# Fifteen 1 MB weight buffers instead of six of 2 MB, in a decoder block with 32 experts

## The chip, the cores and the metric

The kernel runs on one core of one Trainium2 chip. The metric is the device time of one execution in microseconds (us), as the median of several runs.

## What is computed

One decoder block on 512 tokens of width 2048, all in float32. Two attention branches (forgetting attention and chunkwise retention, 8 heads of 128 each) are merged through gates and projected back; a router then picks for each token one group of four, and two of the eight experts in it; each expert is a gated MLP; the sum is normalized. The part that matters here:

```python
h = h + merged @ w_out[l]
hn = rmsnorm(h, norm_ffn_w[l]).reshape(b * s, d)
...
def expert_block(args):
    xi, e = args
    return (jax.nn.silu(xi @ w1[e]) * (xi @ w3[e])) @ w2[e]

yb = lax.map(expert_block, (xb, blk_expert)).reshape(cap, d) * buf_w[:, None]
return jnp.zeros((t_tok + 1, d), h.dtype).at[buf_tok].add(yb)[:t_tok]
...
h = h + moe.reshape(b, s, d)
return rmsnorm(h, norm_final_w)
```

For each expert w1 and w3 are 2048 x 512 and w2 is 512 x 2048, 4 MB each, so the 32 experts have 403 million bytes of weights. The program reads all of them.

## The kernel before

**First stage.** The projections, the branches and the output projection take 120 weight units of 1 MB (128 partitions x 2048 floats). `Stream.unit` loads two units at a time, 2 MB with rows of 16 KB, into one of two buffers of the pool `raw` (L74). ScalarE casts a unit to the high part of a split number (L96), VectorE subtracts to get the low part (L97), both into one of two buffers of 2 MB of the pool `split`; TensorE multiplies high and low parts against activations that are split in the same way (L225 to L244, L477, L593 to L595).

**Router.** The rows of h are transposed and split once more into `hh` and `hl` (L552, L553), TensorE makes the logits from them (L557 the high part, L558 the low), and a chain of small instructions on all engines gives every token its experts and places. `prep` then gathers the tokens of an expert by matmuls with a selection matrix (L720) and writes them to `xs`.

**Expert stage.** An expert has six pieces of 2 MB: four for `gemm1`, each with four k tiles of w1 and of w3 (two rows of 8 KB in a partition), and two for `gemm2`, each with two column blocks of w2 (rows of 16 KB). The program runs gemm1 of expert e, the gather for e + 1, and gemm2 of e - 1, in that order. The pieces go in turn through six buffers: the two of `raw`, the two of `split`, and two of a new pool `raw2`. All loads are issued by SyncE (SP) at L817, in the order in which the program writes them (`manual_schedule` for SP): a load whose buffer is not free holds up all that stand behind it. The other engines are ordered by the scheduler. The result of an expert, 64 rows, goes to `ybuf` in memory with a scatter from GpSimd (L798); the last expert's result stays on chip as `ys`, and `fw` is the final norm's weight on all partitions.

**Combine.** For each of four tiles of 128 tokens SP loads both expert rows of each token from `ybuf` (L925, 2 MB with rows of 16 KB, into the same six buffers). TensorE adds h, the second row and the last expert's (L938 to L941), VectorE adds the first row (L942, and L945 the second row for one column block) into a tile `res`, of which there are two, in the buffers of `raw2`. Then comes the norm: squares on ScalarE (L947), sums and inverse root on VectorE (L951 and L952, L112 to L122), scaling (L957 on VectorE, L959 on ScalarE), and two writes to the output (L962).

After that comes a loop for experts with more than 64 tokens, which calls the same functions.

## Time and profile before

| | us |
|---|---|
| runs, median (lowest to highest of 3) | 2464.65 (2463.22 to 2465.13) |
| profiled execution, whole time | 2461.32 |
| its span in the profile | 2459.5 |
| TensorE busy | 2355.6, 96% of the span |
| VectorE busy | 737.6, 30% |
| ScalarE busy | 488.6, 20% |
| GpSimd busy | 233.4, 9% |
| data moved, whole span | 594.22 MB, mean 242 GB/s |

The busy shares are means over the two stages, the seam at some 1423 to 1454 us between them, and the combine from some 2414 us on, so each stage has to be read by itself. The slices of the page show this at once: data move at 73 to 154 GB/s in slices 2 to 23, and at 414 to 423 in slices 25 to 39. The granted TensorE clock is 0.99 of full speed over the span.

### The profile page before, as it was taken

The numbers are of one execution on the slowest core, as the hardware profiler recorded it, in microseconds if no ns is written. First come the engines' busy times: TensorE is split into PE (matmuls) and PEld (weight loads), VectorE is DVE, ScalarE is ACT, GpSimd is POOL, SyncE is SP. The second block draws the span as 40 slices with busy tenths as digits, with TensorE's granted clock in tenths as the row PEclk, the third lists the DMA queues.
The fourth block names the chain that finished last, engine by engine and source line by source line (L and its number), as shares of the span: only waits on it lengthen the run. The fifth ranks groups of instructions, "written<-read, shape, count | busy, mean of one in ns | idle before, by whom it ended". The sixth has DMA issues, their size and how long they took to land. (4 is left out here: it accounts for less than half of the span.)

```text
span 2459.5 us, 35971 instructions
## 1 busy us (share of the span) xinstructions
PE 2355.6 (96%) x16110; PEld 1605.8 (65%) x16114; DVE 737.6 (30%) x1271; ACT 488.6 (20%) x617; POOL 233.4 (9%) x328
## 2 busy tenths in 40 slices
PE   8999999999999999999999979999988999999986
PEld 6888888888888888888888854544444444444422
DVE  4444445544442222244433231111111111111105
ACT  5222223222222222232223310000010000000013
POOL 0000000100100000001003121111111111111002
PEclk9999999999999999999999989999999999999998
DMA  7233334232223333244432369999999999999996
GB/s 289 98 107 128 108 101 139 79 110 73 107 78 128 128 124 117 109 151 154 146 125 87 146 267 416 414 421 422 422 421 422 422 422 422 421 422 422 422 423 249
DMA packets 85839, 594.22 MB, mean 242 GB/s; under 512 B 7800, under 2 KB 24248, under 8 KB 34640
## 3 DMA queue, kind: packets, MB, share of 16 engines
q1 hardware_dynamic: 56704, 549.48, 55.1%
q0 software_dynamic: 7856, 25.61, 3.1%
q10 hardware_dynamic: 21120, 16.78, 2.1%
q8 instruction: 128, 2.10, 0.3%
q14 instruction: 31, 0.25, 0.0%
HBM read 562.72 MB, written 37.24 MB: 244 GB/s over the span
## 5 line engine op out<-in xcount | busy, mean ns | idle before, releaser
L745 PE MATMUL ab<-wraw,xs 128*64 128x512 f32 x2048 | 461.8, 603 | 39.2 <-DMA wraw<-in_wM_dram 39.0
L225 PE MATMUL acc<-xh,whl 128*128 128x512 f32 x1152 | 453.2, 393 | 0.0
L227 PE MATMUL acc<-xh,whl 128*128 128x512 f32 x1152 | 453.2, 393 | 0.0
L226 PE MATMUL acc<-xl,whl 128*128 128x512 f32 x1152 | 452.7, 393 | 0.0
L96 ACT CAST whl<-wraw 128x2048 fp32r<-128x2048 f32 (+1 forms) x122 | 228.0, 1869 | 780.3 <-PE acc L227 412.4
L745 PEld LDWEIGHTS ab<-wraw,xs 128*64 128x64 f32 x2048 | 144.0, 138 | 325.4 <-issue 252.0
L97 DVE TENSOR_TENSOR whl<-wraw,whl 128x2048 fp32r<-128x2048 f32 (+1 forms) x122 | 275.3, 2257 | 202.2 <-ACT whl L96 201.9
L226 PEld LDWEIGHTS acc<-xl,whl 128*128 128x128 f32 x1152 | 216.4, 188 | 46.4 <-issue 1.4
L225 PEld LDWEIGHTS acc<-xh,whl 128*128 128x128 f32 x1152 | 216.5, 188 | 45.8 <-issue 0.5
L227 PEld LDWEIGHTS acc<-xh,whl 128*128 128x128 f32 x1152 | 216.4, 188 | 45.8 <-issue 1.4
L745 PE MATMUL y<-wraw,gs 128*64 128x512 f32 x1024 | 235.0, 602 | 1.7 <-DMA wraw<-in_wM_dram 1.2
L720 PEld LDWEIGHTS <-h 128*128 128x128 bf16 x6144 | 189.9, 98 | 49.5 <-issue 49.1
L720 PE MATMUL gp<-S,h 128*128 128x64 bf16 x6144 | 199.2, 193 | 1.2 <-issue 1.2
L723 DVE TENSOR_TENSOR xs<-gp,nfw 128x512 f32<-128x512 f32 x64 | 41.9, 688 | 417.0 <-PE ab L745 375.2
L745 PEld LDWEIGHTS y<-wraw,gs 128*64 128x64 f32 x1024 | 69.4, 137 | 119.2 <-issue 114.1
L705 POOL TENSOR_SCALAR S<-slot,rank 128x128 bf16<-128x128 f32 x124 | 73.4, 602 | 705.3 <-PE gp L720 673.8
L758 ACT ACTIVATE ab<-ab,rs 128x512 f32<-128x512 f32 x32 | 22.0, 687 | 524.4 <-PE ab L745 506.7
L242 PE MATMUL acc<-whl,xh 128*128 128x512 f32 x256 | 101.8, 401 | 6.2 <-ACT xh L201 6.2
L795 ACT COPY ysb<-y 64x512 f32<-64x512 f32 x62 | 35.8, 579 | 339.0 <-PE y L745 330.6
L243 PE MATMUL acc<-whl,xh 128*128 128x512 f32 x256 | 102.6, 401 | 0.0
L593 PE MATMUL acc<-whl,mh 128*128 128x512 f32 x256 | 100.4, 392 | 0.0
L594 PE MATMUL acc<-whl,mh 128*128 128x512 f32 x256 | 100.2, 391 | 0.0
(302 smaller groups left out, 2121.6 us busy)
## 6 DMA issues: line engine op xcount, KB each, us to landing
wraw<-in_wM_dram SPq DMA_DIRECT2D x192, 2048.0 KB, 23.7
wraw<-in_wA_dram SPq DMA_DIRECT2D x59, 2048.0 KB, 7.8
ybuf<-zero ACTq DMA_DIRECT2D x8, 1024.0 KB, 5.7
gate<-gs ACTq DMA_DIRECT2D x32, 256.0 KB, 2.0
g<-gate POOLq DMA_DIRECT2D x32, 256.0 KB, 2.9
wraw<-ybuf SPq DMA_DIRECT2D x4, 2048.0 KB, 26.4
xt<-in_x_dram SPq DMA_DIRECT2D x4, 1024.0 KB, 6.4
hc<-in_x_dram POOLq DMA_DIRECT2D x4, 1024.0 KB, 5.5
```

The lines of the kernel that those rows point to most:

```text
L96: nc.scalar.copy(hi[:, c], w[:, c])
L97: nc.vector.tensor_sub(lo[:, c], w[:, c], hi[:, c].bitcast(F32))
L225: nc.tensor.matmul(acc, wh, xh[:, k], start=(k == 0), stop=False)
L226: nc.tensor.matmul(acc, wh, xl[:, k], start=False, stop=False)
L227: nc.tensor.matmul(acc, wl, xh[:, k], start=False, stop=(k == KT - 1))
L242: nc.tensor.matmul(accs[t], xh[:, k, s], wh, start=(k == 0), stop=False)
L243: nc.tensor.matmul(accs[t], xh[:, k, s], wl, start=False, stop=False)
L593: nc.tensor.matmul(accs[t], mh[k][:, s], wh, start=(k == 0), stop=False)
L594: nc.tensor.matmul(accs[t], mh[k][:, s], wl, start=False, stop=False)
L705: i = eng.tensor_scalar(S[:, t], slot1.rearrange("p a b -> p (a b)"), rsel[:, t:t + 1], None, op0=OP.is_equal)
L720: nc.tensor.matmul(gp[:, d], h3[i][:, t, (8 * g + d) * P:(8 * g + d + 1) * P], S[:, t, :SLOTS], start=(t == 0 and i == 0), stop=(t == NT - ...
L745: nc.tensor.matmul(acc[m * SLOTS:(m + 1) * SLOTS], st, w[m], start=first, stop=last)
```

## The change

The memory for weights becomes 15 buffers of 1 MB: four of `raw` (128 x 2048), four of `split` (128 x 2 x 1024), and seven of `raw2` with names of their own, r0 to r6. A unit of the first stage is loaded by itself, 1 MB with rows of 8 KB, and split in two halves of 1024 columns. A piece of an expert is four k tiles of w1 or of w3, or one column block of w2, always 1 MB with rows of 8 KB; the matmuls take two pieces at a time and are themselves the same. From the last expert on, `fw` lies in r0 and `ys` in r1, and the loads go through the other 13 buffers. In the combine the rows of a tile come in two loads of 1 MB, and the sums are made in place in the first row's buffer, so that there is no tile `res`. `fold`, which nothing used, is gone.

```diff
+NR2 = 7
...
-        self.cur, self.half = self.raw.tile([P, 2, 2048], F32, name="wraw"), 0
-        nc.sync.dma_start(self.cur, src_of())
+    def load(self, src):
+        w = self.raw.tile([P, 2048], F32, name="wraw")
+        self.nc.sync.dma_start(w, src)
+        return w
+
+    def parts(self, w, after=None, n=1024):
+        nc, res = self.nc, []
+        for m in range(2):
+            hl = self.split.tile([P, 2, 1024], F32R, name="whl")
+            wm = w[:, m * 1024:(m + 1) * 1024]
...
+                    nc.scalar.copy(hl[:, 0, c], wm[:, c])
+                    nc.vector.tensor_sub(hl[:, 1, c], wm[:, c], hl[:, 0, c].bitcast(F32))
...
-    raw = hold("raw", 2)
-    split = hold("split", 2)
+    raw = hold("raw", 4)
+    split = hold("split", 4)
...
-    fold = rp[0].tile([P, P], F32, name="fold")
-    half = P // 2
-    nc.vector.tensor_add(fold[:, :half], ident[:, :half], ident[:, half:])
-    nc.vector.tensor_add(fold[:, half:], ident[:, :half], ident[:, half:])
...
-    raw2 = scC.enter_context(pool("raw2", 2, reuse_waits="tile"))
+    raw2 = scC.enter_context(pool("raw2", 1, reuse_waits="tile"))
+    slots = [(raw, "wraw")] * 4 + [(split, "whl")] * 4 + [(raw2, f"r{i}") for i in range(NR2)]
+    loads = itertools.cycle(slots)
...
-            w = next(pieces)
+            w = [next(pieces), next(pieces)]
...
-    loads = iter(itertools.cycle([raw, raw, split, split, raw2, raw2]))
...
-    def pieces_of(e, part):
-        for i in range(2 if part else 4):
-            w = piece_tile(next(loads))
-            nc.sync.dma_start(w, (w2 if part else w13)(a["wM"][e], i))
+    def pieces_of(we, part):
+        for q, u in ([(4, 0), (4, 1), (5, 0), (5, 1)] if part else
+                     [(m + g // 2, g % 2) for g in range(4) for m in (0, 2)]):
+            w = buffer()
+            nc.sync.dma_start(w, we[q][:, u * 2048:(u + 1) * 2048])
             yield w
...
-        fw = yp[0].tile([P, D], F32, name="fw")
+        fw = buffer((P, D), F32, "fw", 8)
...
+            ys = buffer((P, D), F32R, "ys", 9)
...
-            yb = piece_tile(next(loads) if first else raw)
-            nc.sync.dma_start(yb, yv[t])
-            return [[yb[:, k, c * T:(c + 1) * T] for c in range(4)] for k in range(2)]
+            ys = [buffer((P, D)) for _ in range(2)]
+            for k in range(2):
+                nc.sync.dma_start(ys[k], yv[t][:, k])
+            return ys
...
-            y0, y1 = ybs[t] if first else load_y(t)
-            r = raw2.tile([P, D], F32, name="res", tag="wraw")
+            r, y1 = ybs[t] if first else load_y(t)
...
-                nc.vector.scalar_tensor_tensor(r[:, cs], y0[c], wtf[:, 0, t:t + 1], pr,
+                nc.vector.scalar_tensor_tensor(r[:, cs], r[:, cs], wtf[:, 0, t:t + 1], pr,
```

**The order, on SP at the seam.** The last load of the first stage and the loads that fill the buffers, before. The names in brackets are the semaphores waited for: PE, DVE, Pool, Activation are the engines; DMAHW0 to 7 count landed transfers of the hardware queues, which take these eight in turn, DMASW those that GpSimd issued.

```order
L74 DMA wraw<-in_wA_dram 128x4096 [waits DMAHW1_49,DVE_49]
L817 DMA wraw<-in_wM_dram 128x2x2048 [waits DMAHW2_49,DVE_49]
L817 DMA wraw<-in_wM_dram 128x2x2048 [waits DMAHW3_49,DVE_49]
L817 DMA wraw<-in_wM_dram 128x2x2048 [waits PE_49] x2
L817 DMA wraw<-in_wM_dram 128x2x2048 [waits DMASW4_49,DMASW5_49,DMASW3_49,DMASW6_49,DMASW2_49,Pool_49]
L817 DMA wraw<-in_wM_dram 128x2x2048 [waits DMASW4_49,DMASW5_49,DMASW3_49,DMASW6_49,DMASW2_49,DMASW7_49,DMASW1_49,DMASW0_49]
L817 DMA wraw<-in_wM_dram 128x2x2048 [waits DMAHW4_49,PE_49]
```

The same place now (L68 and L820 are the loads there).

```order
L820 DMA wraw<-in_wM_dram 128x2048 [waits DMAHW6_49,DVE_49]
L820 DMA wraw<-in_wM_dram 128x2048 [waits PE_49] x4
L820 DMA wraw<-in_wM_dram 128x2048 [waits DMASW3_49,DMASW2_49,DMAHW7_49,DVE_49,PE_49]
L820 DMA wraw<-in_wM_dram 128x2048 [waits DMASW5_49,DMAHW0_49,DMASW4_49,Pool_49]
L820 DMA wraw<-in_wM_dram 128x2048 [waits DMAHW1_49,DMASW6_49,DMASW0_49]
L820 DMA wraw<-in_wM_dram 128x2048 [waits DMAHW2_49]
L820 DMA wraw<-in_wM_dram 128x2048 [waits DMASW5_49,DMASW6_49,DMASW4_49,DMASW7_49,DMASW3_49,DMAHW3_49,DMASW2_49,DMASW1_49]
L820 DMA wraw<-in_wM_dram 128x2048 [waits DMAHW4_49]
L820 DMA wraw<-in_wM_dram 128x2048 [waits DMAHW5_49]
L820 DMA wraw<-in_wM_dram 128x2048 [waits DMAHW6_49,PE_49]
```

Before, the two loads into `raw2` (fifth and sixth) wait only for transfers of the first stage and for GpSimd; now the first of seven (r0, the third row) waits for TensorE and VectorE as well: for the last logits matmul that reads `hl` and the VectorE instruction that writes it, since r0 lies over that memory. r1 to r6 follow, with waits for the landing of the load eight before (DMAHW) and for transfers of the first stage; the last row is the sixteenth load, which waits for the first expert's first matmuls.

**The order, on VectorE in the combine.** From the second tile's scaling to the third tile's sums, before:

```order
L957 SCALAR_TENSOR_TENSOR res<-res,rs_w,fw 128x512 [waits DVE_49]
L957 SCALAR_TENSOR_TENSOR res<-res,rs_w,fw 128x512
L942 SCALAR_TENSOR_TENSOR res<-wraw,wt,ab 128x512 [waits DMAHW1_49,DMAHW0_49,DMAHW6_49,PE_49,Activation_49]
L942 SCALAR_TENSOR_TENSOR res<-wraw,wt,y 128x512 [waits PE_49]
L942 SCALAR_TENSOR_TENSOR res<-wraw,wt,ab 128x512
L942 SCALAR_TENSOR_TENSOR res<-wraw,wt,y 128x512 [waits PE_49]
L945 SCALAR_TENSOR_TENSOR res<-wraw,wt,res 128x512 [waits DVE_49]
```

From the first tile's scaling to the third tile's sums now (L946 and L949 are the sums there, L955, L956, L98 and L99 the second tile's reduction and root, L961 the scaling):

```order
L961 SCALAR_TENSOR_TENSOR wraw<-wraw,rs_w,fw 128x512 [waits DVE_49]
L961 SCALAR_TENSOR_TENSOR wraw<-wraw,rs_w,fw 128x512
L955 TENSOR_REDUCE v_19694<-ss_19659 128x1 [waits Activation_49]
L946 SCALAR_TENSOR_TENSOR wraw<-wraw,wt,ab 128x512 [waits DMAHW6_49,DMAHW3_49,PE_49]
L956 TENSOR_SCALAR v_19694<-v_19694 128x1 [waits DVE_49]
L946 SCALAR_TENSOR_TENSOR wraw<-wraw,wt,ab 128x512 [waits PE_49]
L949 SCALAR_TENSOR_TENSOR wraw<-wraw,wt 128x512 [waits DMAHW4_49,DVE_49]
L98 TENSOR_SCALAR rs_t<-v_19694 128x1 [waits DVE_49]
L946 SCALAR_TENSOR_TENSOR wraw<-wraw,wt,y 128x512 [waits PE_49]
L99 TENSOR_SCALAR rs_w<-rs_t 128x1 [waits DVE_49]
```

Before, the third tile's first sum stands behind the whole second tile and waits for the landing of the first tile's output (two of its DMAHW semaphores); now it stands one tile earlier and waits only for its rows from `ybuf` and for TensorE.

## Rows read from the trace of the kernel before

**Rows 1.** The page, part 1: busy us (share of span) xinstructions:

```profile
PE 2355.6 (96%) x16110; PEld 1605.8 (65%) x16114; DVE 737.6 (30%) x1271; ACT 488.6 (20%) x617; POOL 233.4 (9%) x328
```

**Rows 2.** TensorE waits up to 1415 us: total, times, longest:

```profile
PE acc L242 <- ACT xh L201: 6.2, 1, 6.2
PE acc L477 <- DVE whl L85: 0.6, 1, 0.6
```

**Rows 3.** Expert stage, one window: busy (xcount) per engine, PEclk, DMA share, GB/s:

```profile
1460.00:2400.00 940.00, 877.02 (x9223) 407.37 (x9220) 113.25 (x291) 76.04 (x134) 97.61 (x147) 0.99 1.01 421
```

**Rows 4.** TensorE's waits in the expert stage:

```profile
PE ab L745 <- DMA wraw<-in_wM_dram: 39.0, 28, 1.9
```

**Rows 5.** SP timeline, loads at the seam: start, duration, instruction:

```profile
1404.56 0.37 SPq L817 DMA_DIRECT2D wraw<-in_wM_dram  x1
...
1411.17 0.37 SPq L817 DMA_DIRECT2D wraw<-in_wM_dram  x1
...
1422.98 1.63 SPq L817 DMA_DIRECT2D wraw<-in_wM_dram  x3
...
1453.41 0.37 SPq L817 DMA_DIRECT2D wraw<-in_wM_dram  x1
```

**Rows 6.** Windows at the seam, columns as in rows 3:

```profile
1435.00:1440.00 5.00, 1.07 (x4) 0.93 (x4) 3.85 (x20) 0.09 (x1) 0.52 (x1) 0.50 0.88 365
1440.00:1450.00 10.00, 7.90 (x209) 7.68 (x211) 3.62 (x14) 0.00 (x0) 2.66 (x5) 0.72 0.01 2
1453.00:1456.00 3.00, 3.00 (x16) 1.01 (x14) 0.00 (x0) 0.00 (x0) 0.00 (x0) 1.00 0.53 156
1456.00:1460.00 4.00, 4.00 (x20) 1.29 (x18) 0.00 (x0) 0.00 (x0) 0.00 (x0) 1.00 1.00 424
```

**Rows 7.** Timeline of TensorE: last logits, first expert matmul:

```profile
1434.26 0.41 PE L558 MATMUL lg<-hl,wrs 128*100 128x256 f32 x1
...
1449.72 0.65 PE L745 MATMUL ab<-wraw,xs 128*64 128x512 f32 x2
```

**Rows 8.** DMA view, 1696:1711 and 1726:1741, loads of w1 and w3:

```profile
DMA packets 812, 6.33 MB, mean 422 GB/s; under 512 B 48, under 2 KB 48, under 8 KB 48
...
q1 hardware_dynamic: 810, 6.30, 101.2%
...
DMA packets 809, 6.28 MB, mean 419 GB/s; under 512 B 48, under 2 KB 48, under 8 KB 48
...
q1 hardware_dynamic: 807, 6.25, 100.6%
```

**Rows 9.** DMA view, 1715.7:1721.5 and 1745.7:1751.5, loads of w2:

```profile
DMA packets 229, 2.48 MB, mean 428 GB/s; under 512 B 67, under 2 KB 67, under 8 KB 67
...
q1 hardware_dynamic: 171, 2.40, 97.9%
...
DMA packets 193, 2.47 MB, mean 425 GB/s; under 512 B 38, under 2 KB 38, under 8 KB 38
...
q1 hardware_dynamic: 175, 2.47, 100.0%
q0 software_dynamic: 18, 0.00, 0.2%
```

**Rows 10.** The tail: window from 2431 to 2454, and VectorE's waits in it:

```profile
2431.00:2454.00 23.00, 10.19 (x27) 4.29 (x25) 19.18 (x55) 9.64 (x23) 5.48 (x4) 0.75 0.35 139
...
DVE v L951 <- ACT ab L947: 1.6, 2, 0.8
DVE res L942 <- DMA out_dram<-res: 0.6, 1, 0.6
```

**Rows 11.** The page, part 5: splitting a weight unit on ScalarE and VectorE:

```profile
L96 ACT CAST whl<-wraw 128x2048 fp32r<-128x2048 f32 (+1 forms) x122 | 228.0, 1869 | 780.3 <-PE acc L227 412.4
...
L97 DVE TENSOR_TENSOR whl<-wraw,whl 128x2048 fp32r<-128x2048 f32 (+1 forms) x122 | 275.3, 2257 | 202.2 <-ACT whl L96 201.9
```

**Rows 12.** SP's wait ahead of the loads from ybuf:

```profile
SPq L925 <- DMA ybuf<-ysb,idx: 11.9, 1, 11.9
```

More of the change, by code (lines that the diff above doesn't have):

```diff
@@ new lines, in __init__ @@
+        self.fill = None
+    def load(self, src):
[7 more added lines that the diff above has]
+            wm = w[:, m * 1024:(m + 1) * 1024]
+            with ExitStack() as st:
+                for i in after or ():
+                    st.enter_context(self.tc.issue_after(i))
+                for q in range(1024 // n):
+                    c = slice(q * n, (q + 1) * n)
+                    if self.fill is not None:
+                        self.fill(2 * m + q, w)
+                    nc.scalar.copy(hl[:, 0, c], wm[:, c])
+                    nc.vector.tensor_sub(hl[:, 1, c], wm[:, c], hl[:, 0, c].bitcast(F32))
+            res.append(hl)
+        return res
@@ L149, in unit, with fill, part @@
         pos[0] += 1
-        if k == 0:
-            stream.first(a["wA"][0].rearrange("p (u n) -> p u n", u=2))
-        return stream.unit(lambda: a["wA"][k // 2].rearrange("p (u n) -> p u n", u=2), after)
+        src = a["wA"][k // 2][:, (k % 2) * 2048:(k % 2 + 1) * 2048]
+        if k:
+            hl = stream.parts(stream.load(src), after)
+        else:
+            w = raw.tile([P, 2048], F32, name="wraw")
+            def fill(q, w):
+                c = slice(q * T, (q + 1) * T)
+                nc.sync.dma_start(w[:, c], src[:, c])
+                load_x(0, q)
+            stream.fill = fill
+            hl = stream.parts(w, n=T)
+            stream.fill = None
+        def part(o, n):
+            c = slice(o % 1024, o % 1024 + n)
+            return hl[o // 1024][:, 0, c], hl[o // 1024][:, 1, c]
+        return part
     nmw = consts.tile([P, KT], F32, name="nmw")
@@ L235, in proj_V @@
                 load_x(g)
-            hi, lo = unit(kind, q, g)
+            part = unit(kind, q, g)
             for t in range(NT):
@@ L464, in hybrid_block @@
         for j in range(KT):
-            hi, lo = unit("br", j, after=done[3] if j == 1 else None)
+            part = unit("br", j, after=done[3] if j == 1 else None)
             gs, bs = [], []
@@ L583, in hybrid_block @@
             for g in range(4):
-                hi, lo = unit("wo", c, g)
+                part = unit("wo", c, g)
                 for t in range(NT):
@@ L696, in hybrid_block, with buffer @@
     cp = scC.enter_context(pool("cx", 2, reuse_waits="tile"))
-    raw2 = scC.enter_context(pool("raw2", 2, reuse_waits="tile"))
+    raw2 = scC.enter_context(pool("raw2", 1, reuse_waits="tile"))
+    slots = [(raw, "wraw")] * 4 + [(split, "whl")] * 4 + [(raw2, f"r{i}") for i in range(NR2)]
+    loads = itertools.cycle(slots)
+    kept = set()
+    def buffer(shape=(P, 2048), dtype=F32, name="wraw", slot=None):
+        if slot is not None:
+            kept.add(slots[slot][1])
+        while slot is None:
+            pl, tag = next(loads)
+            if tag not in kept:
+                break
+        else:
+            pl, tag = slots[slot]
+        return pl.tile(list(shape), dtype, name=name, tag=tag)
     gathering = []
@@ L769, in hybrid_block, with gemm2 @@
     yp = []
-    def gemm2(blk, pieces, late=False):
+    def gemm2(blk, pieces, ys=None):
         gs, idx = blk
+        late = ys is not None
         if late:
             wsl, sT = idx
-            ys = yp[0].tile([P, D], F32R, name="ys")
         else:
@@ L779, in gemm2 @@
         for q in range(2):
-            w = next(pieces)
             y = psY.tile([P, DE], F32, name="y")
+            w = [next(pieces), next(pieces)]
             for k in range(4):
-                halves_mm(y, gs[:, k], [w[:, m, k * DE:(k + 1) * DE] for m in range(2)], k == 0, k == 3)
+                halves_mm(y, gs[:, k], [w[m][:, k * DE:(k + 1) * DE] for m in range(2)], k == 0, k == 3)
             for m in range(2):
```

78 lines of the change are left out of this document (16 added, 62 removed).

## The prediction

> **What bounds the kernel now.** I read the busy table first, then the waits of TensorE, then both again by stretch. The page shows TensorE busy for 2355.6 of 2459.5 us [rows 1], which alone would make any change to buffers worthless. By stretch it is two kernels. Up to 1415 us TensorE waits only twice, 6.2 and 0.6 us [rows 2]: no weight load is ever late there. After 1460 us its 877.02 us of work lie in 940 us, while the DMA share is 1.01 and 421 GB/s flow [rows 3]; TensorE's waits between 1475 and 2425 are first of all for weights, 39.0 us [rows 4]. So the expert stage is bound by the DMA engines: it ends when its bytes are in, and only three things can move its end: how many bytes are in before it starts, how fast a byte goes, and what follows the last byte. TensorE has 63 us to spare there.
>
> The seam between the stages is the place of the change. Of the six loads that fill the buffers the second is issued at 1404.56, the third at 1411.17 and the last three from 1422.98 on; the next issue is at 1453.41 [rows 5]. The table of windows shows what that costs: up to 1440 data flow, from 1440 to 1450 nothing does (share 0.01), and from 1453 to 1456 the rate is 156 GB/s, which is 1.1 us at 424 GB/s, so data flow again from 1454.9, 1.5 us after the issue [rows 6]. From 1435 to 1440, 365 GB/s at a rate of some 420 is 4.4 us of flow: the six buffers of 2 MB are full at 1439.4. The DMA engines stand idle for 15.5 us because there is no free buffer; the router (TensorE waits for its chain until the gathers) holds the first expert matmul back to 1449.72 [rows 7].
>
> **The change part by part.** All of it against the profiled execution, 2461.32 us, which is 3.33 below the median of 2464.65.
>
> *Lead.* 15 buffers of 1 MB hold 15.73 million bytes where 6 of 2 MB hold 12.58. The difference of 3.146 MB is loaded ahead if it arrives before the first buffer is released, which is at 1453.41 as before, since a pair of 1 MB pieces feeds the same matmuls as one piece of 2 MB. The order shows when the seven new buffers can start: the first of them waits for a TensorE instruction, the other six stand behind it in SP's queue and wait for nothing late. That instruction is the last logits matmul on `hl`, whose memory the new buffer r0 lies over; in the trace it is the row that starts at 1434.26 and lasts 0.41 [rows 7], so r0 is issued at 1434.7 and flows from 1436.2. The first eight pieces are issued no later than in the kernel before (four at 1404 or earlier, two by 1411, two at 1423) and are in by about 1430. Seven loads are 7.34 MB, 17.4 us at 422 GB/s: in at 1453.6, just before data would flow again at 1454.9. So all 15 are full at the same time at which 12 were before, and from then on every release frees the same bytes as before. Since the DMA engines never pause afterwards, the lead stays to the end: 3.146 MB at 422 GB/s is **-7.5 us**. The bound on the other side is 0: if r0 is issued later than 1436, every microsecond is lost from the lead.
>
> *w2 in rows of 8 KB.* A piece of w1 and w3 already has rows of 8 KB; a piece of w2 had rows of 16 KB, 134.2 MB in all. The nearest rows are windows of the stage in which SP's queue moves only the one kind or the other: 422 and 419 GB/s in 15 us each for 8 KB [rows 8], 428 and 425 in 5.8 us each for 16 KB [rows 9]. I take the means, 420.5 and 426.5, by which 134.2 MB takes 4.5 us longer: **+4.5 us**. The y rows, 8.4 MB, go the same way, +0.3. The bounds: 0, since windows this short differ by packets at their edges, and +7.5 by the queue's own rows, whose bytes by their share (6.30 MB at 101.2%, 6.25 at 100.6%; 2.40 at 97.9%, 2.47 at 100.0%) give 414.6 against 424.5 GB/s. The Trainium skill ("DMA: Bandwidth & Descriptors", Why small descriptors are slow) gives a fixed overhead of about 3 cycles per packet; as an estimate from that page, with its fabric clock of 850 MHz, 512 more rows on each engine would cost 1.8 us, and the sum would be 2.7 us lower. No window here shows so small a difference, so the sum goes by the windows.
>
> *Twice as many loads.* After 1454.9 the kernel issues 377 loads instead of 190, 187 more. Each load brings 16 small packets, one per DMA engine: the window of three loads has 48 under 512 B [rows 8]. A small packet's price stands in the row of q0: 18 packets in 0.2% of 16 engines over 5.8 us [rows 9], 10 ns each. 187 times 10 ns on every engine is **+1.9 us**; bounds 0 and +2.4 (13 ns, by the rounding of 0.2%).
>
> *The tail.* The sums now go into the y0 buffer instead of two `res` buffers, so the third tile need not wait until the first tile's output has been written, and the order shows its five sums right behind the first tile's scaling, with the second tile's inverse root between them. After 2431 VectorE waits 0.6 us for that write and twice 0.8 for ScalarE's last square, ahead of the third and the fourth tile's root [rows 10]. The first two go, the fourth tile's 0.8 stays, since nothing is left to fill it: **-1.4 us**. VectorE is busy 19.18 of these 23 us [rows 10], so the bounds are 0 and -3.0 (3.8 idle less 0.8).
>
> *At nothing.* The first stage's loads and splits come in halves, twice as many: TensorE covers them (a unit's split costs 1.87 us on ScalarE and 2.26 on VectorE [rows 11], of 1415 us over 120 units, 11.8 us each). Without that cover, each unit's split would stand in the path, 4.1 us a unit before as after. The opening wait of 6.2 us is for x, not for weights. `fold` is gone from VectorE, two small sums before the router, at most 0.3 us. From the last expert on r0 and r1 hold `fw` and `ys` and 13 buffers are left; by then TensorE waits for data, buffers are empty, and nothing is late. The y loads still wait 11.9 us for the last scatter [rows 12], but with the 12 MB of the last expert's pieces still to come, 29.8 us of data, that wait costs no byte.
>
> Sum: -7.5 + 4.5 + 0.3 + 1.9 - 1.4 = **-2.2**, so 2459.1 for the profiled execution and **2462.4** against the median. A measurement of this kernel can tell 0.2%, 4.9 us, from no change; this is inside it.
>
> **The rivals.**
> 1. *The lead counts in full.* Rows of 8 KB cost no more than 1 us, and the small packets hide between data: -7.5 + 1 + 0 - 1.4 = -7.9, 2456.8. For it: from 1456 to 1460, with 8 KB rows alone, 424 GB/s flow [rows 6]. Against: in the longer windows the 8 KB rows are the slower ones.
> 2. *Eight loads at a time.* In the order a load waits for the landing of the load eight before it. That is 8 MB under way where there were up to 12: if DMA engines run dry while SP still waits, the stage grows with every expert. 0.25 us in each of 31 experts is 7.8 us, and from there on the change is slower (-2.2 + 7.8 = +5.6); at 0.5 us the time is 2478. Against: 8 MB are 19.9 us of data, and data flow 1.5 us after an issue [rows 5, 6]. For: the landing of a load is counted when its slowest engine is done.
> 3. *The buffers don't fill.* r0 comes late (if the program's new order moves the logits, or an earlier load waits), and the seven loads only follow the first release: lead 0, sum +5.3, 2470. This is the change not doing what it says. Against: the matmul on `hl` is done 15 us before the first expert matmul.
> 4. *A fixed time per load.* The 1.5 us from issue to flow could be paid by each of the 187 loads that are added: 280 us, 2742. Against: 190 such loads are there now, and their bytes at 421 GB/s fill the stage with a share of 1.01 [rows 3], so nothing of it shows between them. The Trainium skill (the same page, Anatomy of one DMA) gives about 2.0 us fixed per DMA; by that rule the time would be more still, and the trace shows it hidden.
>
> **How the numbers follow.** Forecast (a lead of 6 to 7.5, and row and packet prices between half and one and a half of those taken) 0.55, from 2459 to 2467; rival 1 0.29; rival 3 0.08, of which half keeps some of the lead; rival 2 0.07; rival 4 0.01. Faster by over 0.2% is rival 1 with the forecast's lower edge (0.04), 0.33; slower is rivals 2 and 4 and half of rival 3, 0.12; the rest, 0.55, is within 0.2%. The range from 2455.5 to 2469.0 takes in rival 1 with the tail near its bound of -3.0 and the part of rival 3 that keeps some lead; rivals 2 and 4 are left out.
>
> **What would show it.** Right: seven issues at 1434.7, 15 full buffers near 1453.6, no gap of more than 1.5 us in the DMA share there, and the first wait of TensorE for a weight later than before. The stage's rate should fall from 421 to about 418 GB/s; a rate of 421 or more means rival 1. A share under 1.00 between 1500 and 2400 means rival 2; a gap from 1430 to 1454 means rival 3. In the tail no VectorE wait should be for a write of the output. The prediction is wrong if the time up to 1423 us moves by more than 1 us, since nothing in it should.

## The result and the profile after

The change made the kernel slower. The median is 2491.76 us (2488.50 to 2494.03, 4 runs) against 2463.93 for the kernel before (2462.42 to 2465.13, 4 runs): a ratio of 1.0116, interval 1.0103 to 1.0128, or 28 us. The profiled execution took 2491.16 us with a span of 2489.5.

The lead that the change is for did appear. The table of windows of the kernel after, columns as in [rows 3], begins at the seam:

```profile
1436.00:1440.00 4.00, 0.80 (x18) 0.73 (x19) 3.09 (x13) 0.00 (x0) 0.65 (x1) 0.50 1.01 425
1440.00:1450.00 10.00, 10.00 (x210) 7.95 (x209) 2.04 (x7) 0.00 (x0) 4.22 (x8) 0.86 1.02 426
1450.00:1453.00 3.00, 3.00 (x18) 1.00 (x16) 0.00 (x0) 0.00 (x0) 0.00 (x0) 1.00 0.80 227
...
1500.00:1600.00 100.00, 98.08 (x1223) 50.72 (x1220) 11.14 (x25) 6.10 (x11) 8.96 (x14) 1.00 0.93 382
1600.00:1700.00 100.00, 98.16 (x975) 44.60 (x973) 10.45 (x24) 6.68 (x12) 9.86 (x15) 1.00 0.88 360
1700.00:2380.00 680.00, 646.44 (x6308) 290.85 (x6306) 83.95 (x220) 51.56 (x92) 70.03 (x106) 1.00 1.00 413
```

The last three of these windows in the kernel before:

```profile
1500.00:1600.00 100.00, 98.83 (x1296) 52.56 (x1293) 11.98 (x28) 6.69 (x12) 12.45 (x20) 1.00 1.00 415
1600.00:1700.00 100.00, 96.60 (x1089) 46.58 (x1087) 14.83 (x46) 7.76 (x14) 9.88 (x15) 1.00 1.01 421
1700.00:2380.00 680.00, 626.08 (x6251) 281.34 (x6249) 79.37 (x201) 55.95 (x99) 68.82 (x103) 0.99 1.01 422
```

Where the kernel before stood still from 1440 to 1450 with 2 GB/s [rows 6], 426 GB/s flow now. The DMA view counts what SP's queue moves from 1456 to the end (packets, MB, share of 16 engines), before and after, and then from 2380 to the end, before and after:

```profile
q1 hardware_dynamic: 44071, 402.20, 95.8%
q1 hardware_dynamic: 55237, 397.99, 93.4%
...
q1 hardware_dynamic: 2711, 22.08, 66.1%
q1 hardware_dynamic: 5231, 33.81, 74.8%
```

At 1456 the kernel after is 4.2 MB ahead, which is 10.0 us of data at 420 GB/s. At 2380 it is 11.7 MB behind, 27.9 us: that is the 28 us. It lost 15.9 MB between. The three windows hold nearly all of that: the rates differ by 33 GB/s for 100 us, 61 for 100 us and 9 for 680 us, which is 3.3, 6.1 and 6.1 MB. In the last one some 1.4 MB are no pause but the price of smaller rows, since e4 below, with a share of 1.01, moves 420 GB/s there.

So DMA engines that have much left to move are not moving it. The waits of SP's queue say why (line waited at, what for: total, times, longest):

```profile
SPq L820 <- DMA wraw<-in_wM_dram: 364.6, 172, 3.6
SPq L820 <- PE y L758: 260.0, 28, 17.6
SPq L820 <- PE ax L723: 145.0, 24, 27.3
...
SPq L930 <- DMA ybuf<-ysb,idx: 21.1, 1, 21.1
```

The same view of the kernel before, from 1475 to 2380, has no longer wait than this:

```profile
SPq L817 <- PE y L745: 371.6, 59, 10.8
```

Not the totals but the longest waits grew. In the stage a load now waits up to 27.3 us for its buffer; the line of `ax` stands for the small matmul after which TensorE reached the piece in question. The buffers are full and TensorE does not release them in the order in which SP wants them. At the same time TensorE has more to do. From the page: the busy line, two groups of matmuls, and the loads.

```profile
PE 2403.4 (97%) x16110; PEld 1625.8 (65%) x16114; DVE 753.2 (30%) x1388; ACT 511.6 (21%) x735; POOL 225.9 (9%) x328
...
L758 PE MATMUL ab<-wraw,xs 128*64 128x512 f32 x2048 | 507.1, 597 | 13.9 <-DMA wraw<-in_wM_dram 13.7
...
L758 PE MATMUL y<-wraw,gs 128*64 128x512 f32 x1024 | 252.6, 600 | 2.7 <-DVE ysb L806 2.2
...
wraw<-in_wM_dram SPq DMA_DIRECT2D x384, 1024.0 KB, 18.0
```

TensorE is busy 47.8 us longer than before [rows 1] for the same matmuls: `ab` took 461.8 before and `y` 235.0, so together they rose by 62.9 (rows of neighbouring groups overlap, and more so now, so that groups do not add up to the busy time). A stretch of TensorE's timeline shows it (start, duration, instruction, count):

```profile
2053.90 0.47 PE L733 MATMUL gp<-S,h 128*128 128x64 bf16 x10
2054.30 1.07 PE L758 MATMUL ab<-wraw,xs 128*64 128x512 f32 x2
2055.30 0.67 PE L733 MATMUL gp<-S,h 128*128 128x64 bf16 x17
2055.91 3.65 PE L758 MATMUL ab<-wraw,xs 128*64 128x512 f32 x14
```

In `gemm1` and `gemm2` every product is a pair of matmuls (`halves_mm`): one half multiplies from the first of two pieces into one half of the result's rows, the other from the second piece into the other half. Each matmul has two rows in the profile. Four pairs, 16 rows, take 3.65 us when they stand together, 0.91 a pair, because two halves run side by side: in the single rows of the trace the two start 6 to 8 ns apart, and the next two 0.43 to 0.48 us later. Here the first half of the first pair (`x2`) stands alone ahead of a batch of gathers, takes 1.07 us, and the other 14 rows still take 3.65: each second half now starts together with the first half of the next pair, and the last second half (rows at 2058.53 and 2058.96) stands alone. A parted pair costs 1.07 us. There are 42 in `gemm1`, 45 us, which is the whole rise of `ab`, and two in `gemm2`: together 47 of the 47.8 us.

TensorE's order, which the prediction did not look at, had it. Before, a batch of a piece, with the one wait for its load:

```
L745 MATMUL ab<-wraw,xs 64x512 [waits DMAHW6_49]
L745 MATMUL ab<-wraw,xs 64x512 x7
```

After, each half waits for a load of its own, and where the scheduler thought the second one late, it put gathers (`gp`) between:

```
L758 MATMUL ab<-wraw,xs 64x512 [waits DMAHW7_49]
L733 LDWEIGHTS h
L733 MATMUL gp<-S,h 128x64
...
L758 MATMUL ab<-wraw,xs 64x512 [waits DMAHW0_49]
L758 MATMUL ab<-wraw,xs 64x512 x6
```

The same order, followed by pieces, shows the other thing. In load order an expert stands as eight pieces of w1 and w3, then four of w2 of the expert before. After, a few experts into the stage, TensorE takes two pieces of w2, then the eight pieces of the *next* expert, and then the two that are left (64, 65, 68 to 75, 66, 67, by number of the load). Pieces 66 and 67 keep their buffers full meanwhile, the loads into them stand in SP's queue, and all later loads behind them.

Three theories followed. **Parted pairs:** TensorE's longer work is the loss. **Order:** pieces taken out of load order hold up the queue of loads. **Lanes:** the prediction's rival 2, loads that wait for the landing of the load eight before.

### The profile page after: what moved, and what is told of

Read it like the earlier page. It is cut to its first block, busy times and chain, and to the rows that moved or that the text cites. A ratio compares the mean times of both kernels' runs of the same rounds, so it can differ in the third digit from the quotient of the medians.

```text
span 2489.5 us, 36719 instructions
## 1 busy us (share of the span) xinstructions
PE 2403.4 (97%) x16110; PEld 1625.8 (65%) x16114; DVE 753.2 (30%) x1388; ACT 511.6 (21%) x735; POOL 225.9 (9%) x328
## 4 chain that ended last, share of the span: by engine, by line
PE 85%; DMA 11%; issue 2%; DVE 1%; POOL 1%; ACT 0%; SPq 0%; POOLq 0%; DVEq 0%; ACTq 0%
PE ab L758 14%; PE acc L229 11%; PE acc L227 11%; PE acc L228 11%; DMA wraw<-in_wM_dram 10%; PE y L758 7%; PE gp L733 6%; PE acc L244 2%; PE acc L245 2%; PE acc L246 2%; PE acc L477 2%; PE acc L597 2%; PE acc L479 2%; PE acc L595 2%; PE acc L478 2%; PE acc L596 2%
## 5 line engine op out<-in xcount | busy, mean ns | idle before, releaser
L758 PE MATMUL ab<-wraw,xs 128*64 128x512 f32 x2048 | 507.1, 597 | 13.9 <-DMA wraw<-in_wM_dram 13.7
L84 ACT CAST whl<-wraw 128x1024 fp32r<-128x1024 f32 (+1 forms) x242 | 252.2, 1045 | 773.0 <-PE acc L229 419.1
L85 DVE TENSOR_TENSOR whl<-wraw,whl 128x1024 fp32r<-128x1024 f32 (+1 forms) x242 | 296.2, 1226 | 364.0 <-ACT whl L84 361.9
L758 PEld LDWEIGHTS ab<-wraw,xs 128*64 128x64 f32 x2048 | 157.8, 137 | 282.7 <-issue 243.7
L758 PE MATMUL y<-wraw,gs 128*64 128x512 f32 x1024 | 252.6, 600 | 2.7 <-DVE ysb L806 2.2
L733 PE MATMUL gp<-S,h 128*128 128x64 bf16 x6144 | 207.2, 194 | 23.5 <-POOL S L718 16.9
L758 PEld LDWEIGHTS y<-wraw,gs 128*64 128x64 f32 x1024 | 77.3, 138 | 132.5 <-issue 126.6
L808 ACT COPY ysb<-y 64x512 f32<-64x512 f32 x62 | 35.7, 578 | 358.1 <-PE y L758 179.7
L595 PE MATMUL acc<-whl,mh 128*128 128x512 f32 x256 | 100.6, 393 | 0.0
L246 PE MATMUL acc<-whl,xl 128*128 128x512 f32 x256 | 100.4, 398 | 0.0
```

Of the source, the lines that this page charges most:

```text
L84: nc.scalar.copy(hl[:, 0, c], wm[:, c])
L85: nc.vector.tensor_sub(hl[:, 1, c], wm[:, c], hl[:, 0, c].bitcast(F32))
L246: nc.tensor.matmul(accs[t], xl[:, k, s], wh, start=False, stop=(k == KT - 1))
L595: nc.tensor.matmul(accs[t], mh[k][:, s], wh, start=(k == 0), stop=False)
L733: nc.tensor.matmul(gp[:, d], h3[i][:, t, (8 * g + d) * P:(8 * g + d + 1) * P], S[:, t, :SLOTS], start=(t == 0 and i == 0), stop=(t == NT - ...
L758: nc.tensor.matmul(acc[m * SLOTS:(m + 1) * SLOTS], st, w[m], start=first, stop=last)
```

## The experiments

Ratios are against runs of the kernel before on the same chip, whose median lay between 2462.5 and 2463.0. On the texts on record: those that give a pair 0.45 us count one half's share (the rows give 0.91 a pair). The tails that those of e8, e9 and e11 quote (34.7, 37.3, 35.7, 30.4) are each some 10.5 us too short: from the last `y` row to the end the traces show 45.2 us before, 47.8 in e5, 46.3 in e8 and 40.8 in e4. Their differences hold. Line numbers shift a little between kernels.

**e1: the half that waits for the later load goes first**, in the kernel after, so that nothing is left to put between the two.

```diff
-        for m in range(2):
+        for m in (1, 0):
             nc.tensor.matmul(acc[m * SLOTS:(m + 1) * SLOTS], st, w[m], start=first, stop=last)
```

> The changed kernel, with one edit: of the two matmuls of a pair (columns 0 to 63 and 64 to 127) the second half, whose piece is loaded last, is written first. Pair theory: TensorE works on both halves side by side only when they stand next to each other; in the changed kernel each half waits for its own load, so the scheduler puts the first half ahead of gathers that fill the time, and 42 such lone halves of gemm1 take 1.0 us each where the pair takes 0.45. With the late half first both loads are waited for at once and no pair is parted: TensorE busy falls from 2403 to about 2356 us, the expert stage is bound by DMA again, and the time is what the prediction summed up, 2462 (2458 to 2467). Lane theory (eight loads under way at most starve the DMA engines): nothing changes, 2485 or more, with windows of the stage at 360 to 406 GB/s as in the changed kernel. Row theory (8 KB rows and twice as many loads are dear): share 1.01 in all windows, but 408 GB/s or less, 2480 or more.

2479.35 us, ratio 1.0066 (1.0052 to 1.0080): 12.4 of the 28 us came back. TensorE's busy time fell to 2359.9 and no lone half is left. But the windows and SP's waits still show the other loss:

```profile
1500.00:1600.00 100.00, 96.24 (x1274) 50.56 (x1272) 11.14 (x25) 6.10 (x11) 8.96 (x14) 0.98 0.96 389
1600.00:1700.00 100.00, 95.10 (x946) 42.81 (x943) 12.32 (x27) 8.33 (x15) 9.86 (x15) 1.00 0.93 378
```

```profile
SPq L820 <- PE ax L723: 328.3, 29, 23.2
```

Parted pairs are a cause and not the only one.

**e2: the kernel before, each piece in two loads of 1 MB into its two halves.** Six buffers of 2 MB as before, so the same memory, but twice the loads and two waits to a pair.

```diff
-            nc.sync.dma_start(w, (w2 if part else w13)(a["wM"][e], i))
+            src = (w2 if part else w13)(a["wM"][e], i)
+            for m in range(2):
+                nc.sync.dma_start(w[:, m], src[:, m])
```

> The kernel before, with six buffers of 2 MB, but each expert piece comes in two loads of 1 MB, one for each half of the pair. Pair theory: the order shows 36 lone halves, so TensorE gets 25 to 37 us more busy time; since it had 63 us to spare, the time goes up by less, 4 to 20 us (with 6 to 7 us of it from smaller rows of w2 and 190 more loads). Lane theory: 8 MB under way instead of 12, as in the changed kernel, so 25 us or more. Row theory: 20 us or more, with the stage at 412 GB/s or less but a DMA share of 1.01.

2477.93 us, ratio 1.0062 (1.0046 to 1.0077). Two loads to a piece cost 15.3 us, over half of the 28, without any new buffer (some 4.7 of it are the smaller rows of w2, as e10 shows). TensorE is busy 2383.7 us, 28.1 more than before.

**e3: e2 with the late half first.**

```diff
-        for m in range(2):
+        for m in (1, 0):
```

> As the run before, with the late half written first: no pair is parted. This is the kernel before with nothing but smaller rows of w2 and 192 more loads of half the size. By the prediction's prices: 4.5 + 1.9 = 6.4 us slower than before, bounds 0 and 10; TensorE busy as before within 3 us. Lane theory: 25 us or more. If the rows and loads cost nothing: within 2 us of before.

2467.24 us, ratio 1.0018 (1.0009 to 1.0027). e2 less e3 is 10.7 us for parted pairs alone. The windows and SP's waits settle the lanes:

```profile
1600.00:1700.00 100.00, 97.45 (x1095) 47.00 (x1093) 14.82 (x46) 7.64 (x14) 9.85 (x15) 1.00 1.01 419
1700.00:1800.00 100.00, 94.14 (x977) 42.97 (x975) 11.79 (x28) 7.72 (x14) 12.61 (x20) 1.00 1.01 419
```

```profile
SPq L819 <- DMA wraw<-in_wM_dram: 594.3, 276, 3.9
```

SP waits 594.3 us for landings, more than in the kernel after, and the DMA share is 1.01. Rival 2 falls.

**e4: e1 with twelve buffers** instead of 15, the memory of the kernel before.

```diff
-NR2 = 7
+NR2 = 4
```

> The changed kernel with the late half first, and 12 buffers of 1 MB instead of 15 (NR2 = 4). Pair theory with the prediction's lead: 7.5 us slower than the first run here (15 buffers), and bound by DMA. Lane theory: the same as the first run within 2 us, since no more than eight loads are under way anyway.

2462.14 us, ratio 0.9999 (0.9990 to 1.0008): 17.2 us less than e1, by *removing* memory. With twelve buffers the scheduler takes the pieces in load order, and the stage is full again:

```profile
1500.00:1600.00 100.00, 98.94 (x1296) 51.22 (x1294) 12.07 (x28) 6.68 (x12) 12.23 (x19) 1.00 1.01 417
1600.00:1700.00 100.00, 96.30 (x1088) 46.71 (x1086) 14.83 (x46) 7.64 (x14) 9.85 (x15) 1.00 1.01 419
```

The order of pieces depends on the number of buffers, and that order is the second cause. Whether the third megabyte of lead can be had without it was the question of the next runs.

**e5: e1, with the order of loads forced on TensorE**: the matmuls of `gemm1` are issued only after the last `y` of the `gemm2` ahead of them in the queue.

```diff
+            with ExitStack() as st:
+                for i in last_y[-1:]:
+                    st.enter_context(tc.issue_after(i))
...
+            last_y.append(i.ins)
```

> 15 buffers, late half first, and one order more: the matmuls of gemm1 of an expert are issued after the last matmul of the gemm2 written before it, so that TensorE takes the pieces in the order in which SP loads them. Order theory: in the changed kernel, and in the first run with the late half first, the second w2 pair of an expert is multiplied only after most or all of gemm1 two experts on; its two buffers stay full, SP stands before them with later loads behind it, and DMA falls to 378 to 411 GB/s. With load order the DMA share is 1.01 and 415 GB/s or more from 1500 on, SP no longer waits hundreds of us for TensorE's ax, and the lead of 7.5 us shows: 7.5 below the 2462.1 of the 12 buffers, 2455 (2452 to 2459). If more buffers harm in another way (lanes, memory, contention): 2470 or more, as with 15 buffers before.

2468.41 us, ratio 1.0020 (1.0011 to 1.0029): 10.9 us better than e1. SP's wait at `ax` falls from 328.3 to 22.0 us. One dip is left, between 1550 and 1650, at 364 and 402 GB/s. TensorE's timeline shows what it does there:

```profile
1577.23 3.65 PE L758 MATMUL y<-wraw,gs 128*64 128x512 f32 x16
...
1581.36 5.47 PE L733 MATMUL gp<-S,h 128*128 128x64 bf16 x182
1588.44 3.91 PE L733 MATMUL gp<-S,h 128*128 128x64 bf16 x128 [1.61 <-issue]
1594.66 0.98 PE L733 MATMUL gp<-S,h 128*128 128x64 bf16 x15 [2.31 <-issue]
1595.57 4.71 PE L758 MATMUL y<-wraw,gs 128*64 128x512 f32 x16
```

Up to the end of `y` at 1580.9 pieces are released; from then to 1595.6 TensorE only gathers for the next expert, in one lump, and releases no buffer. All buffers are full at that time, so the DMA engines run out of loads some 10 us later:

```profile
1590.00:1600.00 10.00, 7.70 (x112) 4.53 (x110) 0.00 (x0) 0.00 (x0) 0.00 (x0) 0.83 0.42 173
```

Later windows up to 2400, at 419 and 420 GB/s, show no such dip.

**e6: e5 without the late half first**, the order alone.

```diff
-        for m in (1, 0):
+        for m in range(2):
```

> The changed kernel (early half first) with the same order as the run before: pieces are taken in load order, but some 30 pairs are still parted. Pair theory and order theory together: TensorE busy 20 to 30 us above the run before, of which its spare time hides most: 3 to 15 us slower than it, 2458 to 2470. If the order was all of the loss: within 2 us of the run before. If the order was nothing: 2485 or more.

2471.37 us, ratio 1.0033 (1.0021 to 1.0045), 3.0 us more than e5.

**e7: the kernel after with twelve buffers**, early half first.

```diff
-NR2 = 7
+NR2 = 4
```

> The changed kernel with 12 buffers instead of 15 and nothing else (NR2 = 4, early half first): the order shows pieces taken in load order, but 36 parted pairs. Pair theory: against the 12 buffers with the late half first (2462.1) the same loss as between the two runs of the kernel before with two loads, 10.7 us: 2473 (2468 to 2477), TensorE busy 2380 to 2390 us. If parted pairs cost nothing in time: 2462. If the loss of the changed kernel had nothing to do with 15 buffers: 2485 or more.

2470.58 us, ratio 1.0029 (1.0018 to 1.0041), 8.4 more than e4. Parted pairs cost 10.7, 8.4 and 3.0 us in three surroundings, and from the kernel after to e1 12.4: always a cost, and never a fixed one. TensorE's busy time rose by 32.0, 29.3, 22.6 and 43.5 us in these four, so between an eighth and a third of it shows in the time.

**e8: e5 with the last scatter ahead of `dgs` on GpSimd.** In the kernel after SP waits 21.1 us for the last scatter ahead of the y rows, 11.9 before [rows 12], and in GpSimd's order the diagonals `dgs` for the combine stood in front of that scatter.

```diff
-    dgs = diagonals()
+    with tc.issue_after(scatters[-1]):
+        dgs = diagonals()
```

> The run with 15 buffers in load order and late half first (2468.4), with one order more: GpSimd makes the diagonals of the combine (dgs) only after the last scatter is issued. Scatter theory: in that run, as in the changed kernel, dgs stands ahead of the last scatter on GpSimd and waits for TensorE's transposes of the last expert; the loads from ybuf wait for the scatter (SP 19.4 us), the DMA engines fall to 284 GB/s from 2400 to 2430, and the combine ends 37.3 us after the last y matmul where it takes 30.4 with 12 buffers. With the scatter first: 30.5 us, so 7 us less, 2461.4 (2459 to 2464). If the late ybuf rows were for another reason: 2468, SP's wait for the scatter still 15 us or more.

2468.81 us, ratio 1.0022 (1.0013 to 1.0031): no gain. GpSimd's timeline shows the scatter first now, but waiting 33.82 us for VectorE, and VectorE's shows its copies of the result behind `gs` of the last expert, which waits for data:

```profile
2416.41 0.90 POOL L818 DMA_INDIRECT ybuf<-ysb,idx  x1 [33.82 <-DVE ysb L813]
```

```profile
2414.36 0.42 DVE L782 TENSOR_TENSOR gs<-tr,sg 128x256 f32<-128x256 f32 x1 [32.95 <-ACT sg L780]
2414.83 1.30 DVE L813 COPY ysb<-y 64x512 f32<-64x512 f32 x2
```

The theory that `dgs` was the cause fell; it was one engine further up.

**e9: the kernel before with the combine in place**, the only part of the change that touches neither loads nor buffers.

```diff
-            y0, y1 = ybs[t] if first else load_y(t)
-            r = raw2.tile([P, D], F32, name="res", tag="wraw")
+            r, y1 = ybs[t] if first else load_y(t)
...
-                nc.vector.scalar_tensor_tensor(r[:, cs], y0[c], wtf[:, 0, t:t + 1], pr,
+                nc.vector.scalar_tensor_tensor(r[:, cs], r[:, cs], wtf[:, 0, t:t + 1], pr,
```

> The kernel before, and of the change only the combine in place: the sums go into the y0 half of the 2 MB buffer, no tile res. By the tails of the profiles (last y matmul to the end: 34.7 us before, 30.4 with 12 buffers): 4.3 us less, 2458.3 (2457 to 2461). By the prediction's own term, 1.4 us less, 2461.2. If the shorter tail with 12 buffers comes from the smaller y loads: no change, 2462.6.

2457.20 us, ratio 0.9981 (0.9972 to 0.9990): 5.3 us faster than before (2.5 to 6.9 by the interval), where the prediction's bound was 3.0. VectorE's waits from 2414 to 2460:

```profile
DVE ys L791 <- ACT ys L790: 2.5, 1, 2.5
DVE v L950 <- ACT y L946: 0.8, 1, 0.8
```

All the waits of [rows 10] went, 2.2 us, the fourth tile's too, which the prediction had kept; the 0.8 us that stays is the first tile's, ahead of that window. From the last `y` to the end it is 41.3 us against 45.2, 3.9 less. The rest lies in VectorE's rows of that stretch: all its gaps together are 4.2 us against 7.3, its busy time is 31.0 us against 32.5, and what follows its last instruction is 0.7 us longer. Why the same instructions took 1.5 us less in the new order is open.

**e10: the kernel before with w1 and w3 in two loads** (late half first), w2 whole as before: 128 more loads, rows unchanged.

```diff
-        for m in range(2):
+        for m in (1, 0):
...
-            nc.sync.dma_start(w, (w2 if part else w13)(a["wM"][e], i))
+            src = (w2 if part else w13)(a["wM"][e], i)
+            for m in range(1 if part else 2):
+                nc.sync.dma_start(*((w, src) if part else (w[:, m], src[:, m])))
```

> The kernel before with late half first; each w1/w3 piece of 2 MB in two loads of 1 MB, with the same rows of 8 KB; w2 as before, one load with rows of 16 KB. It has the 128 more loads and not the smaller rows. By the prediction's prices (10 ns a load on each engine): 1.3 us slower than before, 2463.9, and the run with w2 in two loads as well (2467.2) then shows 3.4 for rows and 64 loads. If loads are the price and rows are free: two thirds of the 4.65 us, 3.1, so 2465.7.

2462.58 us, ratio 1.0000 (0.9991 to 1.0009). 128 more loads cost 0.1 us, within 2.2 on either side. e3 does the same to w2 also, and so has 64 more loads and rows of 8 KB: it is 4.7 us slower than e10 (2467.24 against 2462.59 of the kernel before beside it, 2462.58 against 2462.50). That is the price of w2 in rows of 8 KB, within some 3 us. SP's queue from 1700 to 2380, in e10 and in e3, agrees:

```profile
q1 hardware_dynamic: 31906, 280.57, 98.6%
q1 hardware_dynamic: 38309, 278.99, 98.8%
```

With the smaller rows it moves 1.6 MB less in 680 us, which is 3.8 us of data or some 5 us over the stage. The kernel before and e9, with w2 in rows of 16 KB, read 280.69 and 280.70 MB, and e4 and e13, with rows of 8 KB, 278.93 and 278.73.

**e11: e8, with VectorE's copies of the result ahead of `gs`.**

```diff
-        last_ins.append(nc.vector.tensor_mul(gs, tr[:, :, SLOTS:], sg))
+        with ExitStack() as st:
+            for i in last_copy[-1:]:
+                st.enter_context(tc.issue_after(i))
+            last_ins.append(nc.vector.tensor_mul(gs, tr[:, :, SLOTS:], sg))
```

> The run with 15 buffers, load order and the last scatter ahead of dgs (2468.8), with one order more, on VectorE: the product gs of an expert is issued after the copies of ysb written before it. In that run the last expert's gs stands ahead of the two last copies and waits 33 us for ScalarE, so the last scatter goes out at 2416 and the rows from ybuf come late. Copies theory: the scatter goes out some 25 us earlier, SP's wait for it falls under 12 us, the combine ends 30.5 us after the last y matmul instead of 35.7, and the time is 5 to 7 us less, 2462 to 2464. If not: 2468 or more, with the scatter still after 2410.

2466.43 us, ratio 1.0014 (1.0005 to 1.0023). It is 2.4 us less than e8, yet the scatter goes out at 2412.82, only 3.6 us earlier than in e8, so the copies theory did not hold either: SP's wait for the scatter is still 19.2 us, and the dip at 1550 to 1600 is there, at 370 GB/s.

**e12: e11 with `gemm2` of the expert before written ahead of the gathers** for the next one, so that the gathers no longer collect into one lump.

```diff
-        if e + 1 < NE:
-            x0 = prep_e(e + 1)
         if 0 < e < NE - 1:
             gemm2(prev, pieces_of(a["wM"][e - 1], 1))
+        if e + 1 < NE:
+            x0 = prep_e(e + 1)
```

> The same with one more order: gemm2 of the expert before is written ahead of the next expert's gather, so the scheduler spreads the gather's matmuls between the pairs of gemm1 instead of in lumps of 10 us and more. Lump theory: while the 15 buffers are full, the DMA engines get only what TensorE releases, so a lump of gathers stops them (375 GB/s from 1550 to 1650 in the run with load order); with an even pace the windows from 1550 to 1700 show 410 GB/s or more, the lead seen at 1456 (3 MB less to load than before) is kept, and the time is 7 us below the run with the copies first, 2455 (2452 to 2458). If the lead is lost in another way while the buffers are full: 2460 or more, with a dip at another place.

2464.88 us, ratio 1.0007 (0.9998 to 1.0016). The stage does what the prediction wanted: from 1475 to 2380 every window reads 417 to 420 GB/s at a share of 1.01, and the last matmul of `gemm1` comes 7.3 us earlier than in e4. It is also this edit that moves the last scatter, to 2384.78; SP waits 2.9 us for it. What was gained is given back at the end. TensorE's timeline there:

```profile
2412.22 2.04 PE L957 MATMUL ab<-wraw,dgs 128*128 128x512 f32 x2 [9.26 <-DMA wraw<-ybuf]
2414.19 9.07 PE L758 MATMUL y<-wraw,gs 128*64 128x512 f32 x32
```

A matmul of the combine, which waits 9.26 us for the y rows, has been put ahead of the last expert's `gemm2`.

**e13: e12, with the combine's matmuls issued after the last `y`.** This and e14 were run because it was open whether that one misplaced matmul is all that hides the lead, and what the lead is worth.

```diff
+                with ExitStack() as st:
+                    for i in last_y[-1:] if first else ():
+                        st.enter_context(tc.issue_after(i))
```

> 15 buffers, late half first and even gathers (2464.9), with one order more: the combine's matmuls are issued after the last y matmul. In the run before, the first tile's matmul on the rows from ybuf stood ahead of the last gemm2 on TensorE and waited 9.3 us, then the clock was at half for the next. Order theory: the last y matmul ends some 11 us earlier, and since the rows from ybuf are then the next bound (last of them in at about 2424), the time falls by 8 to 11 us: 2455 (2453 to 2458), 7 us faster than the kernel before. If the combine is bound by something else: 2461 or more.

2455.20 us (2453.47 to 2456.40), ratio 0.9968 (0.9956 to 0.9980): faster than both kernels, by 7.6 us than the one before and by 36.6 than the one after. Its windows, and the end of its last `gemm2`:

```profile
1475.00:1500.00 25.00, 23.51 (x278) 11.60 (x276) 3.58 (x8) 2.23 (x4) 2.60 (x4) 1.00 1.01 421
1500.00:1600.00 100.00, 98.34 (x1154) 48.15 (x1152) 12.04 (x26) 6.58 (x12) 10.74 (x17) 0.99 1.01 419
1600.00:1700.00 100.00, 96.85 (x950) 43.77 (x946) 13.77 (x43) 7.76 (x14) 9.90 (x15) 0.98 1.01 419
1700.00:2380.00 680.00, 640.63 (x6523) 286.41 (x6521) 83.13 (x206) 51.61 (x95) 71.24 (x107) 0.99 1.01 420
```

```profile
2403.06 8.78 PE L758 MATMUL y<-wraw,gs 128*64 128x512 f32 x32 [0.93 <-DVE gs L785]
```

`gemm2` starts 11.1 us earlier than in e12. TensorE is busy for 640.63 of the 680 us, nearly as long as in the kernel after (646.44), and the DMA engines do not pause: the order in which buffers are released decides here more than TensorE's busy time.

**e14: e13 with twelve buffers.**

```diff
-NR2 = 7
+NR2 = 4
```

> The same kernel as the one before it in this call, with 12 buffers (NR2 = 4). If three more buffers are worth the lead of the prediction: 7.5 us slower than with 15, 2462.5 (2460 to 2465). If the gain came from the order alone and the lead is worth nothing: the same within 2 us.

2464.29 us, ratio 1.0006 (0.9997 to 1.0015). With the same orders forced, three more megabytes of buffers are worth 9.1 us, and the orders without them gain nothing on the kernel before. The 9.1 us are not the lead alone: SP's queue has 398.43 MB left at 1456 in e13 and 401.32 in e14, a lead of 2.9 MB or 6.9 us, but at 2380 the difference is 5.4 MB. With twelve buffers this order loses more afterwards, 399 GB/s from 1600 to 1650 where e13 has 418. Against e4, twelve buffers with fewer orders forced, e13 is 6.9 us faster.

## Why the prediction was wrong

**The step that failed** is in the term of the lead: "a pair of 1 MB pieces feeds the same matmuls as one piece of 2 MB", and from it "from then on every release frees the same bytes as before" and "Since the DMA engines never pause afterwards, the lead stays to the end". The matmuls are the same, but not their order. Two loads to a pair parted the pairs, and 15 buffers let the scheduler put off pieces of w2; both cost releases. Put right (e13), the same change, with the same buffers and the same loads, takes 2455.2 us. Between the two lie 36.6 us, in the order in which the edits were added: 12.4 by the late half first, 10.9 by the load order, 2.0 by the scatter and the copies, 1.6 by the gathers, 9.7 by the combine. These shares hold for that order alone, since parted pairs cost as little as 3.0 us once the load order is right (e6). The last two belong together: the even gathers kept the lead, and the combine hid it.

**The cover that was not there.** "TensorE has 63 us to spare there" was read from one window of 940 us [rows 3]. From 1500 to 1700 the kernel before has TensorE busy for 98.83 and 96.60 of 100 us, so there it has nearly nothing to spare. Its pace is that of the releases, and as long as the buffers are full, that is the pace of the DMA engines too. The lump of gathers in e5 fell into this stretch, and so did the worst windows of the kernel after, 382 and 360 GB/s. That a lead makes such a stretch longer, since whoever has loaded ahead waits for TensorE, is argued here and shown by no run of its own.

**The terms, one by one.** The lead came as described, three microseconds earlier (r0 is issued at 1431.8), and in the kernel that keeps it three more buffers are worth 9.1 us (e13 against e14) or 6.9 (against e4) where 7.5 were forecast. w2 in rows of 8 KB costs 4.7 against 4.5: the short windows were good enough. (Of the bounds of that term the queue's rows of 16 KB give 424.3 GB/s and not 424.5, so 7.4 us for 7.5.) The Trainium skill's overhead per packet ("DMA: Bandwidth & Descriptors", Why small descriptors are slow) had given an estimate of 1.8. Two medians 4.7 us apart, within 3, do not exclude it by themselves, but the 1.6 MB that the queue moves less from 1700 to 2380 (e10), some 5 us over the stage, decide against it. The added loads were forecast at 10 ns for a small packet, 1.3 us for the 128 of e10; they cost nothing that could be measured. The tail in place is worth 5.3 against 1.4, above its bound of 3.0, which counted VectorE's idle time from 2431 to 2454 as all there was to gain and its busy time as given. The fourth tile's wait was to stay "since nothing is left to fill it"; in e9 the third tile's inverse root fills it.

**"At nothing"** failed at the first stage. The last matmul of the stage ends 2.0 us earlier than before and the first gather starts at 1439.67 instead of 1442.58; the prediction had named a shift of 1 us as proof against it. It is no accident of one profile: over the five profiles with the old first stage that end is at 1423.1 on average, over the eleven with the new one at 1421.6. From there to the last logits matmul it takes 11.7 us in each of the five and 10.8 in each of the eleven, 0.9 less where "at most 0.3" was granted. No run here takes either part by itself, so the causes stay open. In the tail no VectorE wait is for a write of the output, as forecast, but the y rows, "that wait costs no byte", came late. The last weights land at 2434.09 and the first load from `ybuf` goes out at 2439.97, so here the wait did cost bytes. SP waited 21.1 us for the scatter, which stood behind `dgs` on GpSimd, and whose data VectorE copied only behind `gs` of the last expert:

```profile
2433.36 2.35 POOL L915 TENSOR_SCALAR dgs<-ident,wt 128x128 f32<-128x128 f32 x4 [30.05 <-PE tr L774]
2435.88 0.93 POOL L811 DMA_INDIRECT ybuf<-ysb,idx  x1 [0.17 <-issue]
```

```profile
2433.64 0.42 DVE L778 TENSOR_TENSOR gs<-tr,sg 128x256 f32<-128x256 f32 x1 [31.50 <-ACT sg L776]
2434.10 1.30 DVE L806 COPY ysb<-y 64x512 f32<-64x512 f32 x2
```

**The rivals.** Rival 3 (the buffers don't fill) is refuted by the 425 and 426 GB/s at the seam; rival 4 (a fixed time per load) by e10. Rival 2 had the right direction, slower, and the right mark to look for, a share under 1.00, which shows between 1500 and 1700, but not the cause: e3 has more waits for landings and a share of 1.01. Of rival 1 the lead came in full, and its free rows fell.

**What stays open.** The measured terms do not add up for the kernels with twelve buffers: rows +4.7, tail -5.3 and the earlier router -2.9 make -3.5 for e4, which measured -0.5. Part of that can be seen: e4 is 1.3 MB ahead of the kernel before at 1456, 3.0 us, and only 0.5 MB at 1500, for its windows from 1460 to 1500 run at 391 and 392 GB/s where the kernel before has 421 and 405. e14 is 2.1 us above e4 with the same buffers, so the forced order may have a price of its own. The intervals, some 2 us to either side each, could hold most of both. Not tried were 13 or 14 buffers and w2 in loads with rows of 16 KB in the kernel with 15.

## What to carry to other kernels

When a change alters loads, waits or buffers, read the new order of every engine that a scheduler orders, the one that frees the buffers first; the diff doesn't show it. Where two instructions run side by side and wait for two loads, write the one with the later load first. A lead in an in-order queue of loads is kept only if the pieces are taken in that order and evenly while the buffers are full, so look for the stretch in which the consumer has no slack, and not at its mean over the stage.

## What was not expected of the hardware

A half matmul that stands alone takes 1.07 us, no less than the share of a whole pair in a batch, 0.91, and the batch gains nothing from having lost it: the seven halves behind it take the 3.65 us of eight, since they pair up anew and the last stands alone. 128 more loads of 1 MB, in a queue that is never empty, cost nothing that can be measured: 0.1 us, within 2.2. And removing one output tile from the combine, the smallest edit of all, gave 5.3 us by itself, more than half of the 9.1 that three megabytes of buffers give.
